# Weights in two parts, side by side: the high and low parts of each weight interleaved element by element

## The chip, the cores and the metric

The kernel runs on one core of a Trainium2 chip. The metric is the time of one execution on the device, in microseconds (us). The engines of the core are TensorE (PE in the rows; PEld for its loads of stationary operands), VectorE (DVE), ScalarE (ACT), GpSimd (POOL) and SyncE (SP), which mostly issues transfers. SBUF, the memory beside the engines, has 128 partitions; a tile has the same layout in each.

## The reference

One inference step of a two-layer decoder for 256 prompt positions and 8 samples (264 columns in all). Layer 0 mixes tokens by dilated sliding-window attention, layer 1 by a complex diagonal state-space layer (S5) with a gated projection; each is followed by a gated feed-forward part with a causal convolution of width 3. Every part stands between two RMS norms.

```python
for i in range(DEPTH):
    ...
    xp = xp + rms_norm(mp, norm_g[i, 1])     # mp: attention or s5_mixer of rms_norm(xp)
    hp = rms_norm(xp, norm_g[i, 2])
    fp, cp = conv_ffn(hp, c0_p, w_up[i], conv_w[i], conv_b[i], w_down[i])
    xp = xp + rms_norm(fp, norm_g[i, 3])

def conv_ffn(h, conv_state, w_up, conv_w, conv_b, w_down):
    u = h @ w_up
    ...
    out = (jax.nn.silu(gate) * val) @ w_down
```

What matters here are the products with the weights: w_qkv (2048 x 9216), w_attn_o (1024 x 2048), w_up (2048 x 11008, per layer), w_down (5504 x 2048, per layer), w_ssm_in (2048 x 2048) and w_glu (2048 x 4096), in fp32.

## The kernel before

All activations are kept transposed: a tile has 128 features in the partitions and the 264 positions as columns. A product with a weight matrix is a sum over blocks of 128 x 128 weights; such a block is the stationary operand of a matmul and 128 x 264 activations are the moving one. The host has put the blocks in the order of their use, eight to a piece of 128 x 1024 numbers (`CB = 8`). There are 772 such pieces in a stream that runs through all eight products (`self.stream`), so that the pieces of one product are fetched while the last one is still at work.

To get nearly fp32 accuracy from matmuls in the type F32R, weights and activations are split into a high part, which is the number in F32R, and a low part, the remainder. `split` (L161 to L163) makes them: ScalarE copies the raw piece into the high part (L162), then VectorE subtracts the high part from the raw piece (L163). A product takes three matmuls (L202 to L204): high weights by high activations, high weights by low activations, low weights by high activations. Each matmul loads its 128 stationary columns anew.

`ensure` (L165) keeps the stream two pieces ahead: when `gemm` begins a piece, it asks for the one after the next. A piece has a raw buffer (four of them, filled by SyncE's queue at L175), a buffer for the high part and one for the low part (three of each, 4 KB per partition). With three buffers, ScalarE's copy for a piece has to wait until TensorE is done with the piece three before it. In a steady stretch a piece is eight blocks of weights and 24 matmuls.

Around the matmuls each product has its own work on the other engines: the evacuation of finished sums (L437 for q, k and v; L743 to L768 for the feed-forward part, L309 for its second product), the attention itself (softmax of the prompt on L659 to L680, the scaling of the probabilities on VectorE in L680, the samples' keys and values on L495 to L617) and, beside the attention, the S5 layer's tables (`s5_setup`, whose instructions all have the line L920; some work on contiguous tiles of 64 numbers, others on arrays in which the numbers lie four elements apart). In the S5 layer ScalarE writes the activations z in another order than it reads them (L1169): `z[:, 0:NP].rearrange("p (c s) -> p s c", s=T4)`, which is every fourth element. L957 and L973 are small matmuls of the tables' preparation beside the first feed-forward part: L957 has 128 stationary and 64 moving columns, L973 has 64 stationary ones.

The order of each engine's instructions is made by the scheduler of the language when the program is built; `later` and `pump` only say before which piece of the stream something is handed to it.

Of the kernel before, what the change touches and what calls it, by code (L numbers as in the profile page):

```python
# [18 lines left out]
F32R = mybir.dt.float32r  # L19
# [7 lines left out]
P = 128  # L27
# [17 lines left out]
CB = 8  # L45
# [78 lines left out]
class Kern:  # L124
# [40 lines left out]
    def ensure(self, i):  # L165

        nc = self.nc
        while len(self.loaded) <= min(i, len(self.stream) - 1):
            n = len(self.loaded)
            raw = self.wp.tile([P, CB * P], F32, tag="wraw", name=self.nm("wraw"), bufs=4)  # L170
            hi = self.wp.tile([P, CB * P], F32R, tag="whi", name=self.nm("whi"), bufs=3)
            lo = self.wp.tile([P, CB * P], F32R, tag="wlo", name=self.nm("wlo"), bufs=3)
            parts = [slice(a, a + 256) for a in range(0, CB * P, 256)] if n == 0 else [slice(0, CB * P)]
            for k, c in enumerate(parts):
                (nc.scalar if k % 2 else nc.sync).dma_start(raw[:, c], self.stream[n][:, c])  # L175
            for c in parts:
                self.split(hi[:, c], lo[:, c], raw[:, c])
            self.loaded.append((hi, lo))
# [1267 lines left out]
```

## Time and profile before

| | before |
|---|---|
| time, median of 3 runs | 2534.07 us (2531.76 to 2534.84) |
| profiled execution, its own time | 2533.61 us |
| span of that execution (first to last instruction) | 2531.8 us |
| TensorE, matmuls | 2465.2 us busy, 97% of the span |
| TensorE, loads of stationary operands | 2437.6 us busy, 96% |
| VectorE | 1788.3 us busy, 71% |
| ScalarE | 1208.4 us busy, 48% |
| GpSimd | 853.9 us busy, 34% |
| DMA | 512.12 MB, 202 GB/s |
[...]

The busy time of an engine counts the time in which at least one of its instructions is under way. Matmuls overlap, and so do the loads. The time of an execution is 1.8 us longer than its span.

### The profile page before, as it was taken

What the parts mean: (1) busy time and instruction counts of PE and PEld (TensorE: products, weight loads), DVE (VectorE), ACT (ScalarE), POOL (GpSimd) and SP (SyncE); (2) the same over time, 40 slices, a digit from 0 to 9 for tenths busy, and PEclk for the clock granted to TensorE, in tenths of its full rate; (3) what the DMA queues carried; (4) which work ended last, traced back from release to release, by engine and by line L of the source; (5) the groups of instructions that cost most, each with busy time, mean ns of one, the idle gap of its engine ahead of it and who ended that gap; (6) DMA issues with size and microseconds to landing.
All of it is one profiled execution on the core that took longest, in us unless ns stands there. A gap on an engine that the chain in (4) does not pass through costs nothing.

```text
span 2531.8 us, 52652 instructions
## 1 busy us (share of the span) xinstructions
PE 2465.2 (97%) x20998; PEld 2437.6 (96%) x20998; DVE 1788.3 (71%) x3002; ACT 1208.4 (48%) x1946; POOL 853.9 (34%) x1153
## 2 busy tenths in 40 slices
PE   8999999999999999999999988999999999999997
PEld 8999999999999999999998988999999999999997
DVE  6788998779888887764446877446877777764444
ACT  5465545556454554443334333444654454443332
POOL 6444448344999980001004564102100000011001
PEclk9999999999999999999999998999999999999998
DMA  7676666665666665565556777555655555566553
GB/s 276 219 258 227 210 221 222 217 222 182 222 214 221 224 211 184 183 205 197 182 183 213 236 233 217 188 183 176 196 179 181 182 180 180 183 205 199 181 182 118
DMA packets 186870, 512.12 MB, mean 202 GB/s; under 512 B 39280, under 2 KB 68992, under 8 KB 186368
## 3 DMA queue, kind: packets, MB, share of 16 engines
q1 hardware_dynamic: 141808, 457.89, 55.4%
q0 software_dynamic: 7968, 26.71, 3.2%
q10 hardware_dynamic: 36848, 24.16, 3.1%
q8 instruction: 164, 2.69, 0.4%
q14 instruction: 82, 0.67, 0.1%
HBM read 469.80 MB, written 38.88 MB: 201 GB/s over the span
## 4 chain that ended last, share of the span: by engine, by line
PE 73%; DVE 11%; issue 4%; DMA 4%; POOL 3%; ACT 3%; ACTq 1%; SPq 0%; DVEq 0%; POOLq 0%
PE ps L204 23%; PE ps L202 23%; PE ps L203 23%; DVE wlo L163 4%; DVE C L752 2%; ACT whi L162 2%; DMA yb<-y 1%; POOL z_room L920 1%; ACTq L953 1%; DMA y<-yb 1%; DVE act L367 1%; DMA ident<-in_ident 1%; DVE act L335 1%; DVE C L755 0%; DVE U L743 0%
## 5 line engine op out<-in xcount | busy, mean ns | idle before, releaser
L202 PE MATMUL ps<-act,whi 128*128 128x264 f32 x6176 | 1771.8, 288 | 10.7 <-ACT whi L162 7.5
L204 PE MATMUL ps<-act,wlo 128*128 128x264 f32 x6176 | 1762.0, 286 | 18.5 <-DVE wlo L163 18.1
L203 PE MATMUL ps<-act,whi 128*128 128x264 f32 x6176 | 1760.7, 285 | 10.0 <-DVE act L335 9.7
L163 DVE TENSOR_TENSOR wlo<-wraw,whi 128x1024 fp32r<-128x1024 f32 (+1 forms) x775 | 978.2, 1263 | 585.3 <-ACT whi L162 584.5
L162 ACT ACTIVATE whi<-wraw 128x1024 fp32r<-128x1024 f32 (+1 forms) x775 | 814.2, 1053 | 894.8 <-PE ps L203 670.5
L204 PEld LDWEIGHTS ps<-act,wlo 128*128 128x128 f32 x6176 | 1168.6, 189 | 23.5 <-DVE wlo L163 23.4
L203 PEld LDWEIGHTS ps<-act,whi 128*128 128x128 f32 x6176 | 1169.0, 189 | 13.7 <-DVE act L335 12.9
L202 PEld LDWEIGHTS ps<-act,whi 128*128 128x128 f32 x6176 | 1165.8, 189 | 16.4 <-ACT whi L162 8.0
L294 POOL TENSOR_TENSOR acc<-acc,sq 128x264 f32<-128x264 f32 x112 | 112.6, 1005 | 669.0 <-ACT sq L300 666.4
L744 POOL COPY ckeep<-U 128x10 f32<-128x10 f32 x172 | 44.8, 261 | 643.7 <-DVE U L743 642.6
L752 DVE SCALAR_TENSOR_TENSOR C<-U,cw,C 128x255 f32<-128x255 f32 (+1 forms) x344 | 197.4, 576 | 0.7 <-ACT C L746 0.7
L746 ACT ACTIVATE C<-U,cw 128x264 f32<-128x264 f32 x172 | 102.3, 597 | 34.8 <-DVE U L743 30.5
L743 DVE TENSOR_TENSOR U<-ps,rstd 128x264 f32<-128x264 f32 x172 | 73.0, 429 | 62.9 <-PE ps L204 62.8
L449 POOL TENSOR_TENSOR qkv<-qkv,cs 32x264 f32<-32x264 f32 x48 | 59.7, 1243 | 123.5 <-DVE sw L443 45.6
L121 POOL TENSOR_TENSOR z_e<-z_pa,z_pb 128x256 f32<-128x256 f32 x64 | 69.1, 1080 | 5.0
L617 ACT ACTIVATE vc<-vc,pk 128x128 f32<-128x128 f32 x192 | 59.5, 390 | 17.2 <-DMA pk<-pd 17.2
L121 POOL TENSOR_TENSOR z_pa<-z_bc,z_tab 128x256 f32<-128x256 f32 x64 | 62.9, 983 | 2.4
L766 ACT ACTIVATE act<-C 128x264 fp32r<-128x264 f32 x86 | 35.5, 413 | 58.7 <-DVE C L764 58.7
L757 ACT ACTIVATE C<-C 128x264 f32<-128x264 f32 x86 | 35.7, 415 | 48.1 <-DVE C L752 44.4
L121 POOL TENSOR_TENSOR z_pb<-z_bc,z_tab 128x256 f32<-128x256 f32 x64 | 56.6, 884 | 0.0
L450 POOL TENSOR_TENSOR sw<-sw,cs 32x264 f32<-32x264 f32 x48 | 51.6, 1075 | 0.0
L668 ACT ACTIVATE S<-S,nmg 128x128 f32<-128x128 f32 (+1 forms) x48 | 21.4, 447 | 61.2 <-DVE nmg L663 61.2
(215 smaller groups left out, 1771.9 us busy)
## 6 DMA issues: line engine op xcount, KB each, us to landing
wraw<-in_w_up SPq DMA_DIRECT2D x344, 512.0 KB, 3.5
wraw<-in_w_down SPq DMA_DIRECT2D x172, 512.0 KB, 3.8
wraw<-in_w_qkv SPq DMA_DIRECT2D x143, 512.0 KB, 4.8
wraw<-in_w_glu SPq DMA_DIRECT2D x64, 512.0 KB, 3.5
wraw<-in_w_in SPq DMA_DIRECT2D x32, 512.0 KB, 3.9
kc<-in_kc SPq DMA_DIRECT2D x24, 512.0 KB, 5.4
vc<-in_vc SPq DMA_DIRECT2D x24, 512.0 KB, 5.9
wraw<-in_w_o SPq DMA_DIRECT2D x16, 512.0 KB, 3.6
```

What stands on the lines that cost most here:

```text
L121: return lambda *a, **k: self.tc.keep_in_program_order(getattr(self.eng, name)(*a, **k))
L162: self.nc.scalar.activation(hi, src, AF.Copy)
L163: self.nc.vector.tensor_tensor(lo, src, hi.bitcast(F32), op=ALU.subtract)
L202: nc.tensor.matmul(o, hi[:, c], xh, start=first, stop=False)
L203: nc.tensor.matmul(o, hi[:, c], xl, start=False, stop=False)
L204: nc.tensor.matmul(o, lo[:, c], xh, start=False, stop=last)
L294: nc.gpsimd.tensor_tensor(st[0], st[0], st[1], op=ALU.add)
L449: nc.gpsimd.tensor_tensor(t[0:ROT, :], t[0:ROT, :], self.cs[:, 0, :], op=ALU.mult)
L617: nc.scalar.activation(vcs[g][:, e], vcs[g][:, e], AF.Copy, scale=pk[:, g, e : e + 1])
L743: nc.vector.tensor_tensor(u, ps[:, 0:NT], rget(), op=ALU.mult)
L746: nc.scalar.activation(c, u, AF.Identity, bias=cw[:, 3, m : m + 1], scale=cw[:, 2, m : m + 1])
L752: nc.vector.scalar_tensor_tensor(c[:, s:NP], u[:, 0 : NP - s], cw[:, j, m : m + 1], c[:, s:NP], op0=ALU.mult, op1=ALU.add)
```

## The change

The high and the low part of a piece are put in one tile of twice the size, in which they alternate: element 0 is the first high part, element 1 the first low part, and so on. `hi` and `lo` become views with a step of two elements. `split` and the three matmuls are the same lines as before, on these views: L162 writes every second element, L163 reads every second element of the tile and writes those between, and the 128 columns of a stationary operand are 128 numbers that lie 8 bytes apart (512 bytes per partition before, 1,024 now from the first to the last). SBUF use is the same: three tiles of 8 KB in place of six of 4 KB.

```diff
--- before.py
+++ after.py
@@ -168,8 +168,8 @@
         while len(self.loaded) <= min(i, len(self.stream) - 1):
             n = len(self.loaded)
             raw = self.wp.tile([P, CB * P], F32, tag="wraw", name=self.nm("wraw"), bufs=4)
-            hi = self.wp.tile([P, CB * P], F32R, tag="whi", name=self.nm("whi"), bufs=3)
-            lo = self.wp.tile([P, CB * P], F32R, tag="wlo", name=self.nm("wlo"), bufs=3)
+            w = self.wp.tile([P, CB * P, 2], F32R, tag="w", name=self.nm("w"), bufs=3)
+            hi, lo = w[:, :, 0], w[:, :, 1]
             parts = [slice(a, a + 256) for a in range(0, CB * P, 256)] if n == 0 else [slice(0, CB * P)]
             for k, c in enumerate(parts):
                 (nc.scalar if k % 2 else nc.sync).dma_start(raw[:, c], self.stream[n][:, c])
```

Since high and low share a tile, its buffer is given back as one. In the built program this moves a wait: before, VectorE's subtraction waited in most pieces for TensorE's last use of the old low part itself; now ScalarE's copy waits for the last matmul of the old piece, and the subtraction waits for the copy and the transfer.

TensorE keeps its order, GpSimd and the queues nearly everywhere. On VectorE and ScalarE some L163 and L162 stand one to eight places elsewhere; two of the larger moves follow. The rows have names of tiles: `wraw` is a raw piece, `whi` and `wlo` its parts (`w` for both after the change), `S` the probabilities of a head and `me` its factors.

VectorE at the softmax of a head of the prompt, beside w_qkv, before:

```order
L590 TENSOR_TENSOR me_4303<-me_4303,z_4346 128x6
L163 TENSOR_TENSOR wlo_4368<-wraw_4366,whi_4367 128x1024
L680 TENSOR_SCALAR S_3995<-S_3995,me_4303 128x128
L680 TENSOR_SCALAR S_3995<-S_3995,me_4303 128x256
L680 TENSOR_SCALAR S_4085<-S_4085,me_4303 128x128
L680 TENSOR_SCALAR S_4085<-S_4085,me_4303 128x256
L680 TENSOR_SCALAR S_4177<-S_4177,me_4303 128x128
L680 TENSOR_SCALAR S_4177<-S_4177,me_4303 128x256
L920 TENSOR_TENSOR z_room<-z_room 128x64 x2
```

The same place with the change:

```order
L590 TENSOR_TENSOR me_4212<-me_4212,z_4254 128x6
L680 TENSOR_SCALAR S_3910<-S_3910,me_4212 128x128
L680 TENSOR_SCALAR S_3910<-S_3910,me_4212 128x256
L680 TENSOR_SCALAR S_3998<-S_3998,me_4212 128x128
L680 TENSOR_SCALAR S_3998<-S_3998,me_4212 128x256
L680 TENSOR_SCALAR S_4088<-S_4088,me_4212 128x128
L680 TENSOR_SCALAR S_4088<-S_4088,me_4212 128x256
L920 TENSOR_TENSOR z_room<-z_room 128x64
L163 TENSOR_TENSOR w_4275<-wraw_4274,w_4275 128x1024
```

The subtraction for the next piece stood ahead of the six L680, and now stands behind them and one L920.

ScalarE in the last heads of the attention, beside w_o (`vc` are values of the samples, `vt` the prompt's values, `pt` its probabilities turned), before:

```order
L162 ACTIVATE whi_6960<-wraw_6959 128x1024
L617 ACTIVATE vc_6943<-vc_6943,pk_6937 128x128 x2
L617 ACTIVATE vc_6945<-vc_6945,pk_6937 128x128 x5
L162 ACTIVATE whi_7017<-wraw_7016 128x1024
L467 ACTIVATE vt_6993<-ps_6990 128x256
```

With the change:

```order
L162 ACTIVATE w_6813<-wraw_6812 128x1024
L617 ACTIVATE vc_6796<-vc_6796,pk_6790 128x128
L617 ACTIVATE vc_6798<-vc_6798,pk_6790 128x128 x6
L467 ACTIVATE vt_6845<-ps_6842 128x256
L162 ACTIVATE w_6869<-wraw_6868 128x1024
```

The copy of the second piece now stands behind L467, the evacuation of the prompt's values, and behind one more L617.

## Rows read from the trace of the kernel before

**Rows 1.** The page, part 1: busy time, share of the span, instructions.

```profile
PE 2465.2 (97%) x20998; PEld 2437.6 (96%) x20998; DVE 1788.3 (71%) x3002; ACT 1208.4 (48%) x1946; POOL 853.9 (34%) x1153
```

**Rows 2.** Groups by shape, costliest first: busy us, mean ns | idle before.

```profile
L202 PE MATMUL ps<-act,whi 128*128 128x264 f32 x6176 | 1771.8, 288 | 10.7 <-ACT whi L162 7.5 <-ACT act L162 3.2
L163 DVE TENSOR_TENSOR wlo<-wraw,whi 128x1024 fp32r<-128x1024 f32 x771 | 976.7, 1267 | 578.7 <-ACT whi L162 577.9
L162 ACT ACTIVATE whi<-wraw 128x1024 fp32r<-128x1024 f32 x771 | 812.8, 1056 | 892.3 <-PE ps L203 670.5 <-issue 168.5 <-DMA wraw<-in_w_qkv 17.6
```

**Rows 3.** Windows: each engine's busy us and instructions, PEclk, DMA share, GB/s.

```profile
321.00:323.60 2.60, 2.60 (x12) 2.60 (x13) 2.57 (x12) 0.00 (x0) 0.00 (x0) 0.50 0.63 192
2230.00:2500.00 270.00, 270.00 (x2235) 270.00 (x2235) 132.20 (x142) 108.88 (x121) 24.68 (x37) 1.00 0.58 190
```

**Rows 4.** Timeline of TensorE, w_up of layer 0: start, us, instruction.

```profile
699.91 0.28 PE L202 MATMUL ps<-act,whi 128*128 128x264 f32 x1
...
702.95 0.28 PE L203 MATMUL ps<-act,whi 128*128 128x264 f32 x1
```

**Rows 5.** Timeline of TensorE, w_qkv.

```profile
321.25 0.42 PE L202 MATMUL ps<-act,whi 128*128 128x264 f32 x1
...
323.67 0.40 PE L204 MATMUL ps<-act,wlo 128*128 128x264 f32 x1
...
325.16 0.37 PE L202 MATMUL ps<-act,whi 128*128 128x264 f32 x1
```

**Rows 6.** Timeline of TensorE's weight loads, S5 preparation.

```profile
637.55 0.97 PEld L957 LDWEIGHTS ps<-z_bd,z_wt 128*128 128x128 f32 x8
```

**Rows 7.** Groups by shape: loads of 128, 64 columns; ScalarE strided, contiguous, short.

```profile
L957 PEld LDWEIGHTS ps<-z_bd,z_wt 128*128 128x128 f32 x128 | 15.6, 192 | 0.0
L973 PEld LDWEIGHTS ps<-z_xk,z_shift 128*64 128x64 f32 x256 | 8.8, 137 | 3.3 <-ACT z_xk L965 1.1
L1169 ACT ACTIVATE z<-y 128x256 f32<-128x256 f32 x16 | 10.7, 672 | 27.5 <-DVE y L1167 21.1 <-DMA ub<-up 6.2
L300 ACT ACTIVATE sq<-act 128x264 f32<-128x264 f32 x60 | 24.5, 414 | 23.1 <-DVE act L1196 19.8 <-DVE act L367 2.7 <-POOL acc L294 0.4
L162 ACT ACTIVATE whi<-wraw 128x256 fp32r<-128x256 f32 x4 | 1.4, 404 | 2.5 <-DMA wraw<-in_w_qkv 2.5
```

**Rows 8.** Instructions of tile wlo: durations in ns, min/median/max.

```profile
L163 DVE TENSOR_TENSOR wlo<-wraw,whi x775: 418/1225/2496, 5.4 to 2504.1; 128x1024 fp32r<-128x1024 f32 x193, 128x256 fp32r<-128x256 f32 x1
```

**Rows 9.** Waits: engine, line, waited for: us in total, times, longest.

```profile
PE ps L204 <- DVE wlo L163: 18.1, 16, 2.4
ACT whi L162 <- PE ps L203: 670.5, 403, 3.6
```

**Rows 10.** Timeline of VectorE: four strided products, eight contiguous ones.

```profile
344.50 0.81 DVE L920 TENSOR_TENSOR z_room<-z_room 128x64 f32<-128x64 f32 x4
...
385.05 1.16 DVE L920 TENSOR_TENSOR z_room<-z_room 128x64 f32<-128x64 f32 x8
```

**Rows 11.** Timeline of VectorE, w_qkv.

```profile
324.49 1.21 DVE L163 TENSOR_TENSOR wlo<-wraw,whi 128x1024 fp32r<-128x1024 f32 x1
325.62 3.04 DVE L680 TENSOR_SCALAR S<-S,me 128x128 f32<-128x128 f32 x6
328.59 0.46 DVE L920 TENSOR_TENSOR z_room<-z_room 128x64 f32<-128x64 f32 x2
```

**Rows 12.** Windows: attention to w_o, w_up of layer 0, all engines.

```profile
0.00:560.00 560.00, 539.38 (x4275) 529.44 (x4276) 462.76 (x1025) 299.12 (x648) 285.15 (x318) 0.99 0.68 228
600.00:1120.00 520.00, 517.67 (x4401) 511.92 (x4400) 422.45 (x602) 267.38 (x402) 323.13 (x415) 1.00 0.64 205
```

**Rows 13.** Windows: the same stretches, VectorE's L163 alone.

```profile
0.00:560.00 560.00, 217.61 (x181) 0.99 0.68 228
600.00:1120.00 520.00, 213.43 (x164) 1.00 0.64 205
```

## The prediction

> **What bounds the kernel now.** I read the page's first part, then the groups by shape, and after those single stretches. [rows 1] has TensorE's matmuls busy in 97% of the span, ScalarE in 48%. [rows 2] shows one of the three gemm lines, 6,176 matmuls; with L203 and L204 it is 18,528. The reader is to see that "mean ns of one" (288) is no pace, since matmuls overlap. The pace is read from starts: in [rows 4] 25 intervals take 702.95 - 699.91 = 3.04 us, 121.6 ns per matmul; over 270 us of the last gemm it is 270 us / 2,235 = 120.8 ns [rows 3]. 18,528 x 121.6 ns are 2,253 of the 2,531.8 us. So the time is a pace, and 1 ns in it is 18.5 us.
>
> What sets the pace? At a granted clock of 0.50 (1.2 GHz) [rows 3] the starts are 220 ns apart (323.67 - 321.25 over 11 intervals [rows 5]), which is 264 columns at 1.2 GHz exactly. At 1.00 (2.4 GHz) 264 columns would take 110 ns, and 121.6 is seen. The extra 11.6 ns doesn't scale with the clock. Nor is it the load: where only 64 columns stream behind loads of 128, the loads follow each other every (0.97 - 0.19) / 7 = 111 ns [rows 6], the last one's own 0.19 us taken off. I take the excess as the speed at which the moving operand can be read: 264 x 4 bytes in 121.6 ns, 8.7 bytes of a partition per ns.
>
> TensorE waits for late weights as well, most of all for the low part: 18.1 us in 16 waits [rows 9].
>
> **The change part by part.** No instruction is added or removed; the tile's two halves get a step of two elements, for the writers and the readers.
>
> *Loads of stationary operands (18,528).* No row has a strided load, so I bound it from both sides. Now 128 columns take 192 ns as recorded and 64 take 137 [rows 7]: 0.86 ns per column, 110 ns for 128, against 111 from load to load. So 1 ns is overhead, or 5 if a column takes one cycle of 1.2 GHz, 0.83 ns. Strided, a load walks over 1,024 bytes. What such a walk costs is seen on three engines. The moving operand does 8.7 bytes per ns: 118 ns for a load. ScalarE's writes at every fourth element (L1169, 256 elements, 672 ns) against 414 ns for 264 in a row [rows 7] cost (672 - 414 + 7) / 256 = 1.03 ns more per element, on top of the 0.85 ns of (1,056 - 404) / 768 [rows 2, 7]: 1.88 ns for 16 bytes, 8.5 bytes per ns, 120 ns. VectorE's products in the S5 setup (L920) [rows 10]: eight on contiguous operands take 1.16 us, 0.136 us apart, so four would take 0.61; four with every fourth element read or written take 0.81. That is 0.05 us more per 64 elements, 0.78 ns, over 1.05 ns ((1,225 - 418) / 768 [rows 8]): 1.83 ns for 16 bytes, 117 ns. With the overhead a strided load takes 118 to 125 ns, where the stream beside it needs 121.6. The middle fits just below the stream, and I take 0; the bounds are 0 and (125 - 121.6) x 18,528 = 63 us. What hides the load is the matmul before it, and the cover becomes thin: of 10 ns to spare next to none is left.
>
> *High copies on ScalarE (772 blocks, 1,056 ns each).* A walk of 8,192 bytes at 8.5 per ns takes 964 ns, where 1,024 x 0.85 = 870 are needed now: +0.09 us each, 72 us in all. ScalarE, busy for 1,208.4 of 2,531.8 us [rows 1], has room for it. *Low parts on VectorE:* 964 ns are less than the 1,075 that 1,024 elements at 1.05 ns need anyway: 0.
>
> [...]
>
> *Waits.* High and low share a buffer now. ScalarE's copy, which waits longest for the last L203 [rows 9], has to wait for the L204 behind it, one matmul or 0.12 us, while VectorE's subtraction, which had to see its own buffer free, waits for the copy alone. Behind the copy on ScalarE stand the stage's activations, and VectorE waits for it. This costs where weights are late already: (0.12 + 0.09) us x 16 waits = 3.4 us at most, 0 at least if those waits come from VectorE's own queue; I take 2.
>
> *Order.* In the printed VectorE rows the subtraction moves behind six L680 and one L920. In the trace it begins at 324.49 us, ahead of them [rows 11]; the six last from 325.62 to 328.59 and one L920 about 0.2 us. So the low part would begin at 324.49 + 2.97 + 0.2 = 327.7 and be there 1.2 us later, at 328.9. The block before it starts on TensorE at 325.16 [rows 5]; 24 matmuls and two more of 121.6 ns on, at 328.3, the low part is due. New wait: 0.6 us. The same pattern recurs once, at the next head. The printed ScalarE rows move a copy behind one small activation (L467); with three buffers a copy starts two blocks, 48 x 121.6 ns = 5.8 us, ahead of its use, which hides it. I take 1 us for the order, with some us either way.
>
> Sum, against the profiled execution's own 2,533.61 us (0.5 below the median of 2,534.07): 2,533.6 + 0 + 2 + 1 = **2,537 us**, +0.1%. A measurement of this kernel can tell about 0.2% (5 us) from no change.
>
> **The rivals.**
>
> *Slower, the load becomes the limit.* Above 121.6 ns each ns of the load is 18.5 us. With ScalarE's walk and the large overhead (125 ns) the time is 2,537 + 63 = 2,600; two streams of nearly equal pace may also hold each other up, by as much again at most: 2,660. For it: the thin cover. Against: the middle of the bounds lies inside. 0.27.
>
> *Slower, heavy.* (a) If moving and stationary reads share one path, 66 + 32 pieces of 16 bytes take 121.6 ns now, 1.24 ns each, and 66 + 64 will take 161: +40 ns, 3,270 us. (b) If any step over one element makes each read cost 16 bytes of walk, a load takes 128 x 1.84 ns + 3 = 238 ns: +117 ns, 4,700 us. For (a): the unexplained 11.6 ns. Against it: its 1.24 ns matches nothing, while 1.84, the moving stream alone, stands beside 1.88 and 1.83. Nothing speaks against (b) but that the steps seen are four elements wide. 0.16 for both. [...]
>
> *Slower, VectorE becomes the bound* though the loads stay hidden: with 1.88 ns per element each subtraction takes 0.85 us more. By stage [rows 12, 13]: 462.8 + 181 x 0.85 = 617 in 560 us, and 422.5 + 164 x 0.85 = 562 in 520, together 99 us over even if VectorE never idled there: 2,636 at least. It decides from 1.6 ns per element on. 0.05.
>
> *Faster.* If the 11.6 ns come from the two read streams colliding at certain addresses, another layout could take them away: 18,528 x 11.6 ns = 215 us, down to 2,322. Or the new order removes some of the waits, 18 us at most [rows 9]. More bytes walked speak against the first, the late low part above against the second. 0.10.
>
> **How the numbers follow.** Forecast 0.42, and it is the one case within 0.2%. Faster 0.10; slower 0.27 + 0.16 + 0.05 = 0.48. The forecast is the likeliest single case, so its 2,537 is the time; slower as a whole is a little likelier. The range, 2,528 to 2,660, holds the forecast, the load as the limit, VectorE as the bound, and a better order down to 2,528; it leaves out the heavy case (0.16) and the rest of the faster one (0.04). The forecast's own range is 2,530 to 2,540.
>
> **What will show it.** Right: starts of matmuls 120.8 to 122 ns apart, L162 at 1.06 to 1.15 us, L163 near 1.23, waits for weights near 18 us. Wrong: another interval. Up to 130 ns the load is the limit; near 160 it is a shared path; near 240 every element pays. If the interval holds and the time doesn't, an L163 of 2 us says VectorE. What I can't bound well is how a load reads steps of two elements; if the prediction fails, it fails there.

## The result, and the profile after

The change makes the kernel slower by 0.8%.

| | before | after |
|---|---|---|
| time, median | 2532.91 us (2531.30 to 2534.84, 4 runs) | 2553.83 us (2552.84 to 2554.23, 4 runs) |
| ratio, with its 95% interval | | 1.0082 (1.0064 to 1.0099) |
| profiled execution: own time, span | 2533.61 us, 2531.8 us | 2552.84 us, 2551.1 us |
| mean granted TensorE clock | 0.989 | 0.991 |

So 20.9 us were lost, where the forecast had 3 and "no change" as the likeliest case. 2553.83 lies in the range (2,528 to 2,660), on the side of the rival "the load becomes the limit".

The page's first part, after (against [rows 1]):

```profile
PE 2486.4 (97%) x20998; PEld 2459.9 (96%) x20998; DVE 1788.0 (70%) x3002; ACT 1275.1 (50%) x1946; POOL 853.4 (33%) x1153
```

VectorE is as busy as before (1788.0 us), ScalarE 67 us busier, and TensorE still busy for 97% of a longer span. The groups by shape, after (against [rows 2] and [rows 7]; busy us, mean ns of one, idle before):

```profile
L202 PE MATMUL ps<-act,w 128*128 128x264 f32 x6176 | 1786.7, 290 | 11.8 <-ACT w L162 8.6 <-ACT act L162 3.2
L202 PEld LDWEIGHTS ps<-act,w 128*128 128x128 f32 x6176 | 1213.3, 197 | 17.7 <-ACT w L162 9.5 <-ACT act L162 3.4
L163 DVE TENSOR_TENSOR w<-wraw,w 128x1024 fp32r<-128x1024 f32 x771 | 975.1, 1265 | 608.0 <-ACT w L162 607.3
L162 ACT ACTIVATE w<-wraw 128x1024 fp32r<-128x1024 f32 x771 | 885.8, 1151 | 840.8 <-PE ps L204 629.6 <-issue 161.6 <-DMA wraw<-in_w_qkv 12.1
```

A copy on ScalarE takes 1,151 ns instead of 1,056, a subtraction on VectorE 1,265 instead of 1,267, and the duration recorded for a load is 197 ns, where it was 189 before:

```profile
L202 PEld LDWEIGHTS ps<-act,whi 128*128 128x128 f32 x6176 | 1165.8, 189 | 16.4 <-ACT whi L162 8.0 <-ACT act L162 3.4
```

Those are durations; the pace of TensorE is in the windows. The same 270 us of the last gemm, after (against [rows 3]; the columns are those of that group):

```profile
2230.00:2500.00 270.00, 270.00 (x2200) 270.00 (x2199) 133.59 (x151) 116.80 (x124) 22.95 (x38) 1.00 0.59 188
```

2,200 matmuls where there were 2,235, with the clock at 1.00 in both: 122.7 ns each instead of 120.8. The pace of the whole run is best taken from all starts: the mean distance from one start to the next within the three gemm lines, at full clock, over the distances within 7% of their median (some 18,000). It was 121.51 ns and is 122.80: +1.29 ns. Over some 18,200 distances at full clock these are 23.5 us. In the stretches at 0.50 the distance is 220 ns, as before, and there was less of them (48.0 us instead of 56.1). At full pace those 8.1 us hold as much in 8.1 x 121.5 / 220 = 4.5 us, which gives 3.6 us back. 23.5 - 3.6 = 19.9 us, and the span grew by 19.3. So nearly all of the loss is in the pace, a little in each matmul; no stage and no wait need be looked for. The waits (against [rows 9]; engine, line, waited for: us in total, times, longest) say the same, first those of TensorE, then those of ScalarE:

```profile
PE ps L204 <- DVE w L163: 17.2, 16, 3.1
PE ps L202 <- ACT w L162: 8.6, 4, 5.4
```

```profile
ACT w L162 <- PE ps L204: 629.6, 401, 3.2
```

ScalarE's copies wait for L204 now, as the shared buffer makes them. TensorE's waits for low parts are 17.2 us against 18.1, and all its listed waits add up to 48.8 us against 50.9: nothing was added.

### The profile page after: what moved, and what is told of

Its sections match the earlier page's. It is cut to its first block, busy times and chain, and to the rows that moved or that the text cites. A ratio compares the mean times of both kernels' runs of the same rounds, so it can differ in the third digit from the quotient of the medians.

```text
span 2551.1 us, 52606 instructions
## 1 busy us (share of the span) xinstructions
PE 2486.4 (97%) x20998; PEld 2459.9 (96%) x20998; DVE 1788.0 (70%) x3002; ACT 1275.1 (50%) x1946; POOL 853.4 (33%) x1153
## 4 chain that ended last, share of the span: by engine, by line
PE 70%; DVE 14%; issue 5%; DMA 4%; ACT 3%; POOL 2%; ACTq 1%; SPq 0%; DVEq 0%; POOLq 0%
PE ps L202 23%; PE ps L204 23%; PE ps L203 22%; DVE w L163 5%; DVE C L752 3%; ACT w L162 2%; DMA yb<-y 2%; ACTq L953 1%; DVE C L755 1%; DVE act L367 1%; DVE U L743 1%; DVE act L768 1%; DMA ident<-in_ident 1%; DMA y<-yb 1%; DMA ub<-up 0%
## 5 line engine op out<-in xcount | busy, mean ns | idle before, releaser
L202 PE MATMUL ps<-act,w 128*128 128x264 f32 x6176 | 1786.7, 290 | 11.8 <-ACT w L162 8.6
L204 PE MATMUL ps<-act,w 128*128 128x264 f32 x6176 | 1775.1, 288 | 17.6 <-DVE w L163 17.2
L203 PE MATMUL ps<-act,w 128*128 128x264 f32 x6176 | 1769.7, 287 | 11.8 <-DVE act L335 11.5
L163 DVE TENSOR_TENSOR w<-wraw,w 128x1024 fp32r<-128x1024 f32 (+1 forms) x775 | 976.6, 1261 | 615.0 <-ACT w L162 614.3
L162 ACT ACTIVATE w<-wraw 128x1024 fp32r<-128x1024 f32 (+1 forms) x775 | 887.2, 1148 | 843.6 <-PE ps L204 629.6
L204 PEld LDWEIGHTS ps<-act,w 128*128 128x128 f32 x6176 | 1219.4, 197 | 22.5 <-DVE w L163 22.0
L203 PEld LDWEIGHTS ps<-act,w 128*128 128x128 f32 x6176 | 1217.8, 197 | 14.8 <-DVE act L335 14.3
L202 PEld LDWEIGHTS ps<-act,w 128*128 128x128 f32 x6176 | 1213.3, 197 | 17.7 <-ACT w L162 9.5
L617 ACT ACTIVATE vc<-vc,pk 128x128 f32<-128x128 f32 x192 | 59.5, 392 | 15.6 <-DMA pk<-pd 15.5
```

The lines of the kernel that those rows point to most:

```text
L162: self.nc.scalar.activation(hi, src, AF.Copy)
L163: self.nc.vector.tensor_tensor(lo, src, hi.bitcast(F32), op=ALU.subtract)
L202: nc.tensor.matmul(o, hi[:, c], xh, start=first, stop=False)
L203: nc.tensor.matmul(o, hi[:, c], xl, start=False, stop=False)
L204: nc.tensor.matmul(o, lo[:, c], xh, start=False, stop=last)
L617: nc.scalar.activation(vcs[g][:, e], vcs[g][:, e], AF.Copy, scale=pk[:, g, e : e + 1])
```

## The experiments

**Which half of the change costs.** Two kernels have a step of two on one side only. In the one, ScalarE and VectorE write two contiguous halves of the tile, and only the loads read every second element; in the other, ScalarE and VectorE work on every second element, and the loads read 128 numbers in a row. In both the weights that a load fetches are others than those meant, so the sums differ from the reference's; kinds and numbers of instructions are the same.

```diff
-            w = self.wp.tile([P, CB * P, 2], F32R, tag="w", name=self.nm("w"), bufs=3)
-            hi, lo = w[:, :, 0], w[:, :, 1]
+            w = self.wp.tile([P, 2 * CB * P], F32R, tag="w", name=self.nm("w"), bufs=3)
+            hi, lo = w[:, 0 : CB * P], w[:, CB * P :]
...
-            self.loaded.append((hi, lo))
+            v = w.rearrange("p (n r) -> p n r", r=2)
+            self.loaded.append((v[:, :, 0], v[:, :, 1]))
```

> Only TensorE's loads have the step of two: ScalarE and VectorE write high and low parts in two contiguous halves of the tile, and the loads take every second number from them (so the stationary operands are a mixture of high and low parts of other blocks). If the loads are all of the loss: 122.8 ns between starts, L162 back at 1056 ns, time 1.008 of before (2553). If the slower copies and the later waits matter: pace 122.8 ns, but time at least 4 us below the changed kernel's.

The other one:

```diff
-            self.loaded.append((hi, lo))
+            v = w.rearrange("p n r -> p (n r)")
+            self.loaded.append((v[:, 0 : CB * P], v[:, CB * P :]))
```

> Only the writers have the step of two: ScalarE and VectorE write interleaved, TensorE loads contiguous columns from that tile (again a mixture of high and low parts). If the loads are all of the loss: 121.5 ns between starts, L162 at 1150 ns, time within 0.2% of before. If the copies and waits matter: 121.5 ns and up to 4 us, 0.15%, more; if strided writes disturb TensorE's reads: a pace above 122 ns.

Measured beside the kernel before (2534.55 us, 17 runs): strided loads 2551.75 us, ratio 1.0070 (1.0056 to 1.0083); strided writers 2538.78 us, ratio 1.0019 (1.0009 to 1.0029). The 270 us of the last gemm, first with strided loads, then with strided writers:

```profile
2230.00:2500.00 270.00, 270.00 (x2199) 270.00 (x2198) 133.90 (x151) 108.34 (x123) 23.96 (x38) 1.00 0.58 188
```

```profile
2230.00:2500.00 270.00, 270.00 (x2233) 270.00 (x2233) 134.21 (x149) 116.45 (x123) 24.22 (x38) 1.00 0.58 191
```

The whole change of pace is there with strided loads alone (2,199 matmuls; 122.79 ns over the run) and none of it with strided writers (2,233; 121.52 ns), though ScalarE writes there as it does in the change (in this window its 123 instructions take 116.45 us, and 108.34 where only the loads are strided). So loads account for +17.2 of some 21 us. Since the pace is that of before, the +4.2 us of the writers are most likely waits: TensorE's waits add up to 58.5 us in that trace (of one of the longer executions, 2543.04 us), and to 50.9 both before and with strided loads. The rows that differ most, first of the kernel with strided writers, then of the one with strided loads:

```profile
PE ps L203 <- DVE w L163: 27.6, 21, 5.9
```

```profile
PE ps L203 <- DVE w L163: 6.4, 5, 1.8
```

L203 is here the first of the three matmuls. With strided writers its load reads from both parts, so it needs the subtraction two matmuls earlier than in the change. The change has 17.2 us of these waits at L204; a part of the 4.2 us is therefore the experiment's own. With strided loads it is the other way: the first four blocks of a piece read only from the high half and the last four only from the low half, so the subtraction is needed later, and this wait is 6.4 us. The sum of the waits, 50.9 us as before, says that the +17.2 us are the pace all the same. What copies and waits cost in the change itself lies between 0 (by the account above) and 4 us.

**What a load costs by itself.** All matmuls of a sum but the first are cut to 256 or 128 columns, in the kernel before and in the one after. With 128 columns the stream should take half as long, so that the load is what remains. The columns left out are not summed, so the outputs are not the reference's. The edit is the same for both layouts:

```diff
-            nc.tensor.matmul(o, hi[:, c], xh, start=first, stop=False)
-            nc.tensor.matmul(o, hi[:, c], xl, start=False, stop=False)
-            nc.tensor.matmul(o, lo[:, c], xh, start=False, stop=last)
+            n = slice(0, NT if first else 128)
+            nc.tensor.matmul(o[:, n], hi[:, c], xh[:, n], start=first, stop=False)
+            n = slice(0, 128)
+            nc.tensor.matmul(o[:, n], hi[:, c], xl[:, n], start=False, stop=False)
+            nc.tensor.matmul(o[:, n], lo[:, c], xh[:, n], start=False, stop=last)
```

> Kernel before with all matmuls but the first of each sum cut to 256 columns (the other 8 columns are left out of these sums). Both theories: the moving stream still sets the pace, 256/264 of 121.6 = 118 ns between starts; a contiguous load, 111 ns, stays hidden.

> Changed kernel with the same cut to 256 columns. If the strided load is the limit, the pace stays where it is with 264 columns, 122.8 ns, 5 ns above the contiguous kernel with the same cut. If the load is short but disturbs the moving stream (about 1 ns per matmul), the pace falls with the columns to 119 ns.

> Kernel before with all matmuls but the first of each sum cut to 128 columns (the other 136 columns left out). The stream needs some 60 ns, so the contiguous load sets the pace: 111 ns by the loads seen in the S5 preparation.

> Changed kernel with the same cut to 128 columns. If the strided load is the limit of the changed kernel, the pace is that of the load by itself and equals the one with 264 columns: 120 to 123 ns, some 10 ns above the contiguous kernel with this cut. If it only disturbs the stream, the load by itself stays at 111 to 113 ns.

The times, of one execution each: 2495.82 us (256 columns, contiguous), 2518.48 (256, step of two), 3921.03 (128, contiguous), 3932.68 (128, step of two). 250 us of the last gemm with 256 columns, contiguous, then with a step of two:

```profile
2200.00:2450.00 250.00, 250.00 (x2119) 250.00 (x2119) 125.21 (x134) 103.17 (x116) 24.00 (x36) 1.00 0.62 197
```

```profile
2200.00:2450.00 250.00, 250.00 (x2082) 250.00 (x2082) 127.91 (x146) 110.98 (x118) 22.31 (x37) 1.00 0.61 194
```

A 128-column stretch of TensorE at full clock, contiguous: the window with its granted clock, then the first matmul of a run without a pause and the 95th after it.

```profile
2404.00:2414.00 10.00, 10.00 (x92) 10.00 (x91) 3.83 (x5) 4.91 (x8) 0.00 (x0) 1.00 0.44 130
```

```profile
2403.68 0.27 PE L205 MATMUL ps<-act,whi 128*128 128x128 f32 x1
...
2414.29 0.34 PE L203 MATMUL ps<-act,whi 128*128 128x264 f32 x1
```

The same place with a step of two, the first matmul and the 91st after it:

```profile
2414.20:2424.20 10.00, 10.00 (x87) 10.00 (x87) 4.29 (x5) 5.46 (x7) 0.00 (x0) 1.00 0.40 116
```

```profile
2413.95 0.28 PE L206 MATMUL ps<-act,w 128*128 128x128 f32 x1
...
2424.69 0.34 PE L203 MATMUL ps<-act,w 128*128 128x264 f32 x1
```

10.61 us / 95 = 111.7 ns against 10.74 us / 91 = 118.0 ns; over all distances at full clock (some 3,500 each) 111.65 and 118.34. A load at a step of two therefore takes 118.3 ns, 6.7 more than a contiguous one, and is still shorter than the stream's 121.5. The reading that the load had become the limit would have left 122.8 at 256 columns too; there the pace is 120.17 ns over the run (before's layout 118.27), so that reading falls. But one in which a load below the stream costs nothing falls as well: at 264 columns the load is below it and costs 1.29 ns. The other reading, a load as short as before that only disturbs the stream, has missed too: it asked for 119 ns at 256 columns and for 111 to 113 at 128.

**Steps of four and eight.** The halves (quarters) of a piece are interleaved too, so that high parts lie four (eight) elements apart; the loads, copies and subtractions all have that step. The sums are the reference's. The edit for four:

```diff
+            w = self.wp.tile([P, 512, 4], F32R, tag="w", name=self.nm("w"), bufs=3)
+            v = w.rearrange("p n (h r) -> p r h n", r=2)
+            hi, lo = v[:, 0], v[:, 1]
...
+            rv = raw.rearrange("p (h n) -> p h n", h=2)
+            for j in range(2) if n == 0 else [slice(0, 2)]:
+                self.split(hi[:, j], lo[:, j], rv[:, j])
...
+            q, j = (i % CB) // 4, (i % CB) % 4
...
+            nc.tensor.matmul(o, hi[:, q, c], xh, start=first, stop=False)
...
```

> High and low parts of two halves of a piece interleaved, a step of four elements for writers, the subtraction and the loads; same tile size, same arithmetic. If a load is limited by the bytes it walks over (2,048 per partition at 8.7 per ns), it takes 236 ns and some overhead: 240 ns between starts, 4,700 us in all; L162 and L163 near 2.1 us each (1.88 ns per element). If a load has only a thin extra cost per strided element (1 ns in 128 per step), some 125 ns and 2,600 us.

> The same with a step of eight elements. If bytes walked count: twice that of step four, 475 ns between starts, 9,000 us. If 16-byte pieces touched count: one piece per element as with step four, the same 240 ns and 4,700 us, L162 and L163 as with step four.

4549.48 and 4692.40 us, one execution each. 500 us of the last gemm with a step of four, then with a step of eight:

```profile
3900.00:4400.00 500.00, 500.00 (x2140) 500.00 (x2140) 209.46 (x169) 195.27 (x129) 25.61 (x40) 1.00 0.31 100
```

```profile
3900.00:4400.00 500.00, 500.00 (x2072) 500.00 (x2071) 230.67 (x215) 201.17 (x143) 22.26 (x47) 1.00 0.29 96
```

233.6 and 241.3 ns per matmul (over the run 233.93 and 241.61): here the load is the limit. The copies are not, since a piece has 24 matmuls, 5.6 us of loads, and its copy takes 2.1. ScalarE's copies, in the groups by shape, with a step of four and of eight:

```profile
L162 ACT ACTIVATE w<-wraw 128x1024 fp32r<-128x1024 f32 x771 | 1590.0, 2062 | 2245.4 <-PE ps L207 1803.5 <-issue 424.7 <-ACT S L671 10.1
```

```profile
L162 ACT ACTIVATE w<-wraw 128x1024 fp32r<-128x1024 f32 x771 | 1649.7, 2140 | 2320.2 <-PE ps L207 1866.0 <-issue 439.5 <-ACT S L671 9.1
```

Going from two to four doubles the load (118.3 to 233.9 ns) and nearly doubles the copy; going from four to eight, with twice as many bytes walked over, adds 3% and 4%. VectorE's subtraction goes from 1,265 to 2,084 and 2,201 ns. The expectation by bytes walked wanted 475 ns at a step of eight, that of a thin extra cost 125 ns at four; both missed, and the one by pieces wanted 240. The time of a load thus doesn't follow the bytes walked over (1,024, 2,048 and 4,096 per partition for 118.3, 233.9 and 241.6 ns). The number of pieces of 16 bytes touched, 64, 128 and 128, fits it at 1.85, 1.83 and 1.89 ns each; that the load reads such pieces is the author's reading, and no run shows it.

**Is it nearness or a disturbance?** Left open was how a load of 118.3 ns costs 1.3 ns beside a stream of 121.5. Either two unsteady steps of nearly equal length hold each other up now and then (A), or a strided load disturbs the stream beside it at any length (B). The moving operand was widened to 288 and 320 columns, so that the load is 14 and 29 ns shorter than the stream.

```diff
-            o = acc[m][:, 0:NT]
-            nc.tensor.matmul(o, hi[:, c], xh, start=first, stop=False)
+            o = acc[m][:, 0:288].rearrange("p (r n) -> p r n", r=2)
+            bh, bl = [x[:, 0:144].unsqueeze(1).to_broadcast([P, 2, 144]) for x in (xh, xl)]
+            nc.tensor.matmul(o, hi[:, c], bh, start=first, stop=False)
...
```

> The kernel before, with the moving operand of all matmuls of a sum but the first widened from 264 to 288 columns: its first 144 columns stand twice and the others are left out, so the sums are not the reference's. It is the partner of the run with loads at a step of two. Both theories: the stream alone sets the pace, 121.5 ns x 288/264 = 132.6 ns at full clock, a load at 111.7 ns lies far below it.

> The kernel after, with the same moving operand of 288 columns. Theory A, two nearly equal rates: the loads (118.3 ns one after another) cost only where their jitter goes past the stream's time; at 132.6 ns the stream is 14 ns longer, so the pace is that of the partner within 0.3 ns. Theory B, the strided load disturbs the stream that runs beside it: each matmul is still slower than the partner's by 1.3 ns or more, about 134 ns.

> The kernel before, with the moving operand widened to 320 columns in the same way (160 columns twice, the others left out). Both theories: 121.5 ns x 320/264 = 147.3 ns at full clock.

> The kernel after, with the same moving operand of 320 columns. Theory A: the pace of the partner within 0.3 ns, since the stream is 29 ns longer than the load. Theory B: still 1.3 ns or more above the partner, about 148.6 ns.

2714.74 and 2728.11 us (288), 2976.43 and 2986.99 us (320), one execution each. A window late in the last gemm with 288 columns, contiguous, then with a step of two:

```profile
2400.00:2670.00 270.00, 270.00 (x2040) 270.00 (x2039) 117.20 (x119) 98.16 (x107) 23.35 (x34) 1.00 0.55 176
```

```profile
2400.00:2670.00 270.00, 270.00 (x2025) 270.00 (x2024) 119.74 (x127) 105.23 (x109) 21.83 (x34) 1.00 0.55 175
```

With 320 columns, contiguous, then with a step of two:

```profile
2650.00:2920.00 270.00, 270.00 (x1832) 270.00 (x1831) 101.56 (x96) 87.19 (x93) 22.40 (x31) 1.00 0.50 159
```

```profile
2650.00:2920.00 270.00, 270.00 (x1823) 270.00 (x1823) 102.53 (x100) 92.76 (x93) 20.98 (x31) 1.00 0.49 158
```

2,040 against 2,025 matmuls, 1,832 against 1,823: a little slower in both. The pace over whole runs, taken as above:

| columns streamed | loads contiguous, ns | step of two, ns | difference |
|---|---|---|---|
| 128 (the load is the limit) | 111.65 | 118.34 | 6.69 |
| 256 | 118.27 | 120.17 | 1.90 |
| 264 (this kernel) | 121.51 | 122.80 | 1.29 |
| 288 | 132.90 | 133.52 | 0.62 |
| 320 | 147.41 | 148.19 | 0.78 |

Neither theory's number came: A wanted at most 0.3 ns at 288 and 320, B at least 1.3. Over whole runs it looks like both in part: a difference of 0.6 to 0.8 ns is left at either width, and on top of it comes one that grows as the two lengths near each other, about 0.6 ns at 264 columns and 1.2 at 256. But the difference is not the same in all stages. Taken over eighths of the matmuls it is 1.7 to 2.1 ns at 256 columns, 0.9 to 1.9 at 264, 0.3 to 0.9 at 288 and 0.0 to 1.2 at 320. So it is shown that the cost is larger where the load is nearly as long as the stream; that a constant part stays at any length is not. An estimate for the part that grows: the distances spread by 2.2 to 2.4 ns where the stream alone sets them (before, and 256 columns contiguous) and by 1.9 where the strided load does. Were each an independent step and the longer of two draws counted, the mean would rise by 0.2 ns at 264 columns and 1.2 at 256; with a constant 0.7, 0.9 and 1.9, where 1.3 and 1.9 were measured. That is argued and not shown. Where the rest, some 0.7 ns, comes from stays open: no run here tells contention between the two reads from a fixed cost of a strided load that the stream doesn't hide. At the clock of 0.50 nothing of it is seen: 220 ns at 264 columns and 240 at 288 with either layout, within 0.2 ns.

## Why the prediction missed its case

**What bounds the kernel: right.** The pace was read as the speed of the moving operand, and the widths fit that: from 264 to 320 columns the contiguous pace rises by 25.9 ns, 0.4625 per column, and 264 x 0.4625 = 122.1 against 121.5 seen. So the pace is proportional to the columns; that reading them is what limits it, and no other step per column, no run separates. The prediction's 1.2 GHz are the 264 columns in 220 ns of [rows 5], 1.2 per ns at a granted clock of 0.50, and its 2.4 GHz are twice that; at 1.00 the kernel before has 264 columns in 121.51 ns, 2.17 per ns. 1 ns of pace for 18.5 us held for the matmuls at full clock (1.29 ns, 23.5 us), of which the shorter stretches at half clock gave 3.6 back.

**Loads: the failed step.** "The middle fits just below the stream, and I take 0; the bounds are 0 and (125 - 121.6) x 18,528 = 63 us." The load itself was priced well: 118 by the moving operand's speed, and 118.3 measured, at the lower end of 118 to 125. What failed is the 0 drawn from it. A load 3 ns below the stream was counted as hidden; it cost 1.29 ns per matmul, some 20 us of the span and inside the bounds. The prediction saw that "two streams of nearly equal pace may also hold each other up", but put that only into the rival in which the load is already the longer one. It belonged into the main sum: with a cover of 3 ns, zero was the end of the range and not its likely place. That the measured time lies in the stated range is owed to this rival's share of it, and not to the sum.

**Copies and subtractions: right.** "+0.09 us each" was 0.095 (1,056 to 1,151 ns), hidden by ScalarE's idle time (840.8 us of it stand before its copies, and with strided writers alone the pace is 121.52 ns, that of before); VectorE 0 was 1,267 to 1,265. The step of two costs 95 ns on a copy and 6.7 ns on a load (111.65 to 118.34).

**Waits and order: mis-sized, both near 0.** "+2" was 17.2 against 18.1 us; each piece now takes TensorE 24 x 1.29 = 31 ns longer, which may also give the copies time. The place where the order was predicted to add a wait of 0.6 us, VectorE's rows after (against [rows 11]), and the matmul that needed the low part:

```profile
331.08 3.12 DVE L680 TENSOR_SCALAR S<-S,me 128x128 f32<-128x128 f32 x6
334.12 0.21 DVE L920 TENSOR_TENSOR z_room<-z_room 128x64 f32<-128x64 f32 x1
334.26 1.21 DVE L163 TENSOR_TENSOR w<-wraw,w 128x1024 fp32r<-128x1024 f32 x1
```

```profile
335.52 0.40 PE L204 MATMUL ps<-act,w 128*128 128x264 f32 x1 [0.26 <-DVE w L163]
```

The wait is there, 0.26 us long, and it is lost in a total that fell.

**The rivals.** "The load becomes the limit" had the right part and the right sign but neither its condition (the load stays below the stream) nor its price (2,600). "Slower, heavy" (b) is wrong at a step of two and right at four: 233.9 ns against its 238. (a), one path for both reads, falls: with 66 + 64 pieces it asked for 161 ns, and the pace is 122.80. VectorE as the bound and a faster kernel did not come.

## What to carry to other kernels

Count the 16-byte pieces that an access pattern touches, multiply by some 1.84 ns, and compare with the time that the instruction takes for its elements in a row (here 0.85 ns per element on ScalarE, 1.10 on VectorE, 111.65 ns for a load's 128 columns). In these runs the larger of the two, with a part of some 140 to 190 ns on VectorE and ScalarE that the elements don't explain, is about what it took; elsewhere it is an estimate to be tested. A hidden step was not free here: the load cost 1.1% of the pace with 3% to spare (264 columns), and 0.5% with 11 to 20% to spare (288 and 320). Put such a share into the sum, times the number of repetitions. To learn whether a cover is thin, shorten and lengthen it on both versions: the differences at several widths said more than any single run.

## What the runs showed that was not expected

**About 1.84 ns for each piece of 16 bytes fits three engines.** Moving operand: 121.51 ns / 66 pieces = 1.84, and 147.41 / 80 = 1.84. Loads: 118.34 / 64 = 1.85 with a step of two, 233.93 / 128 = 1.83 with four, 241.61 / 128 = 1.89 with eight. ScalarE, less the 186 ns that a copy takes apart from its elements (404 - 256 x 0.85, [rows 7]): (1,151 - 186) / 512 = 1.88 and (2,062 - 186) / 1,024 = 1.83, and (2,140 - 186) / 1,024 = 1.91 with eight. VectorE lies a little higher: its subtraction takes 422 ns for 256 elements and 1,267 for 1,024, so 1.10 ns per element and 140 apart from them; (2,084 - 140) / 1,024 = 1.90 with a step of four, and 2.01 with eight. The moving operand is contiguous in all runs, so for it the piece is one way to put 0.46 ns per column, and not shown as its unit. A contiguous load has 32 pieces, 59 ns, and takes 111.65 for its 128 columns, so there it does not show.

**With 128 columns the clock stood at half for most of the run,** though TensorE's matmuls were busy for 98% of it; the page's row of the granted clock, in 40 slices, of the contiguous one:

```profile
PEclk9766667855555555555555668965555555555555
```

The mean is 0.58, and the kernel with half the columns takes 3,921 us instead of 2,534. The two longest stretches at 0.50 last 1,372 and 1,344 us. Each began in or right behind a pause of TensorE, of 1.9 and 1.3 us, and between the matmuls inside them there is less than 0.5 us of pause in all. What would have raised the clock there stays open. At half clock matmuls are 213.3 ns apart there with either layout, where 128 columns at the pace of 220 ns for 264 would need 107. If it is the load that sets the 213.3, as it does at full clock, the step of two costs it nothing there because its own time is longer than the 118 ns of its pieces.
